# Smaller weight units, Silu in one instruction and a third seven-product pair in the feed-forward of a two-layer trunk

## The chip, the cores and the metric

The kernel runs on one core of a Trainium2 chip. The metric is the device time of one execution in microseconds (us), the median of several runs. The engines of the core work side by side, each through its own queue in order: TensorE (PE: matmuls; PEld: the loading of the stationary operand, which overlaps them), VectorE (DVE), ScalarE (ACT), GpSimd (POOL) and SyncE (SP), whose queue issues nearly all transfers from memory here.

## The reference

A decoder trunk of two layers over 256 tokens, width 2048, everything in 32-bit floats. Layer 0 mixes by an mLSTM and a Mamba-2 group, layer 1 by attention; each is followed by the same kind of feed-forward, which the change concerns:

```python
D_MODEL, SEQ = 2048, 256
D_FF = (8 * D_MODEL + 3 * 256 - 1) // (3 * 256) * 256      # 5632

def swiglu(x, w_gate, w_up, w_down):
    return (jax.nn.silu(x @ w_gate) * (x @ w_up)) @ w_down

for layer in range(DEPTH):
    xn = rms_norm(x, norm_mix[layer])
    if layer % 2 == 0:
        x = x + mixer_mlstm_ssd(xn, *mixer_params[layer])
    else:
        x = x + mixer_moba(xn, *mixer_params[layer])
    x = x + swiglu(rms_norm(x, norm_ffn[layer]), *ffn_params[layer])
return rms_norm(x, final_norm)
```

## The kernel before

**Numbers.** TensorE gets its operands in a reduced 32-bit form (`F32R`). Each operand is split into a high part (a cast, on ScalarE) and a low part (operand minus high part, a subtraction on VectorE), and each product is made of three matmuls: high x high, high x low, low x high (`add`, lines 396 to 398). Weights go through this too: a raw tile lands in memory on chip, ScalarE writes `wh`, VectorE writes `wl` (lines 368 and 370).

**Tiling of the feed-forward.** The 5632 hidden columns are 11 strips of 512. They go in parts of 4, 4 and 3 strips. For each strip of a part, `hidden` makes gate and up (one *hidden block*), applies the gate and turns the result over by transposes into `hT`. After the strips of a part, `down` multiplies `hT` with the matching rows of the down weights and adds into the residual `xr_`, in two *down blocks* (q = 0 and 1) of 1024 output columns each.

**Pairs.** A block (`block`) runs over pairs of 128-row tiles of the weights: 8 pairs in a hidden block and in a down block of a four-strip part, 6 in a down block of the three-strip part. A pair multiplies two halves of the tokens (128 each) with two strips of 512 columns over two row tiles: a 2 x 2 by 2 x 2 block product. A letter in a plan says how a pair is done. `P`, plain: 8 products, 24 matmuls into four PSUM banks `F`. `S`, seven products (Strassen-Winograd): 21 matmuls, some into `F`, some into four further banks `E`. It needs sums and differences of the four weight tiles (lines 377 to 380, on VectorE) and of the activations (`activation_sums`), each with its own split. The plans before are `PLAN_X` = PSPSPSPP for hidden blocks, PSPSPPPP and PSPSPP for down blocks of parts of 4 and 3 strips. After the last S of a block the four `E` banks are combined on VectorE into `pre`; in a hidden block `F` is then added to it, in a down block both are added to the residual (line 870).

**Buffers.** `weights` takes units from rings: a unit holds four weight tiles (one pair over two strips), 8 KB in each of the 128 partitions. There are four raw units and three each of `wh` and `wl`. A seven-product pair takes two raw units (one for the sums) and two of `wh` and `wl`, a plain pair one of each. A unit is used again when its last reader is through; the transfer into a raw unit, on SP's queue, waits for that.

**The gate.** Silu is made as tanh on ScalarE (line 857) and two VectorE instructions (858, 859), with the normalization's factor in them.

**Order.** Each engine's instruction order is fixed when the program is built, from the order of the code and from priorities (`tc.high_priority`). Deferred work (`later`, `tick`), such as the transposes of a hidden strip, runs after a pair, and not between the first and the last S of a block (`held`), when the `E` banks are taken.

## Time and profile before

| What | us |
|---|---|
| median of 3 runs (2606.25 to 2607.76) | 2606.94 |
| profiled execution, first to last instruction | 2605.5 |
| TensorE busy in it | 2577.1 |
| VectorE busy | 2043.3 |
| ScalarE busy | 1422.6 |
| feed-forward of layer 0, about 790 to 1500 | 710 |
| feed-forward of layer 1, about 1890 to 2595 | 705 |

The profiled execution is 1.4 us shorter than the median. In the rows of the profile "idle before" is the time in which an engine stood, and the arrow names what ended it. `acc_f` and `acc_e` are the banks `F` and `E`, `x` and `skx` the activations of a hidden block and their sums, `ha` or `hb` and `skh` those of a down block (first and second layer). A view of stretches gives, for each stretch of time, the busy time and count of instructions of each engine, the granted TensorE clock, the share of the DMA engines and the rate.

### The profile page before, as it was taken

How to read it: one execution, taken by the hardware profiler on the slowest of the kernel's cores; microseconds unless marked ns; L12 is line 12 of the kernel's file. 1: busy time of each engine (PE TensorE's matmuls, PEld its weight loads, DVE VectorE, ACT ScalarE, POOL GpSimd, SP SyncE). 2: the span in 40 equal slices, each digit the busy share in tenths (PEclk: the TensorE clock that was granted, in tenths of full speed). 3: DMA queues.
4: the chain of work that ended last, by engine and by line, in shares of the span. 5: the costliest groups of instructions: out<-in, count | busy, mean ns of one | idle time of the engine just before them, and what ended most of it. 6: DMA issues, size and time to landing. Idle time of an engine off the chain costs nothing.

```text
span 2605.5 us, 32598 instructions
## 1 busy us (share of the span) xinstructions
PE 2577.1 (99%) x12255; PEld 2143.7 (82%) x12255; DVE 2043.3 (78%) x2568; ACT 1422.6 (55%) x1886; POOL 46.9 (2%) x97
## 2 busy tenths in 40 slices
PE   8999999999999999999999999999999999999998
PEld 7888888888887888888888788888888888888886
DVE  6676777755548998899889865666699988998898
ACT  5466665565445654555455555566555545554554
POOL 2000010000000000000000000000000000000000
PEclk9999999999999999999999999999999999999999
DMA  7566676566655566565656455555556555565554
GB/s 228 177 184 185 178 236 189 167 186 214 189 173 192 196 200 206 176 216 189 209 173 215 162 170 177 178 171 180 191 173 223 189 199 186 202 215 184 200 193 153
DMA packets 254766, 496.66 MB, mean 191 GB/s; under 512 B 15705, under 2 KB 16097, under 8 KB 254353
## 3 DMA queue, kind: packets, MB, share of 16 engines
q1 hardware_dynamic: 250816, 484.57, 57.6%
q0 software_dynamic: 2896, 8.51, 1.2%
q8 instruction: 96, 1.57, 0.2%
q10 hardware_dynamic: 896, 1.52, 0.2%
q14 instruction: 62, 0.50, 0.1%
HBM read 492.39 MB, written 2.14 MB: 190 GB/s over the span
## 4 chain that ended last, share of the span: by engine, by line
PE 96%; DVE 2%; DMA 1%; ACT 1%; issue 0%; SPq 0%; POOL 0%; ACTq 0%; POOLq 0%; DVEq 0%
PE acc_f L397 14%; PE acc_f L396 14%; PE acc_f L398 14%; PE acc_w L305 11%; PE acc_a L347 8%; PE acc_a L349 8%; PE acc_a L348 8%; PE acc_w L309 6%; PE acc_e L396 3%; PE acc_e L397 3%; PE acc_e L398 3%; PE p_tr L223 2%; PE p_y L776 1%; DMA raw<-in_l_ffn_down 0%; PE p_num L653 0%; DVE wl L290 0%
## 5 line engine op out<-in xcount | busy, mean ns | idle before, releaser
L290 DVE TENSOR_TENSOR wl<-raw,wh 128x1024 fp32r<-128x1024 f32 (+1 forms) x385 | 469.7, 1220 | 335.1 <-ACT wh L289 331.1
L368 ACT CAST wh<-raw 128x1024 fp32r<-128x1024 f32 (+1 forms) x438 | 480.0, 1139 | 345.6 <-PE acc_f L398 284.7
L370 DVE TENSOR_TENSOR wl<-raw,wh 128x1024 fp32r<-128x1024 f32 (+1 forms) x438 | 571.7, 1329 | 66.7 <-ACT wh L368 64.2
L289 ACT CAST wh<-raw 128x1024 fp32r<-128x1024 f32 (+1 forms) x385 | 403.1, 1047 | 389.6 <-PE acc_a L349 172.9
L397 PE MATMUL acc_f<-wl,x 128*128 128x512 f32 x1012 | 394.4, 390 | 0.5 <-DVE wl L370 0.4
L398 PE MATMUL acc_f<-wh,x 128*128 128x512 f32 x1012 | 394.7, 390 | 0.0
L396 PE MATMUL acc_f<-wh,x 128*128 128x512 f32 x1012 | 393.1, 391 | 1.1 <-ACT wh L368 1.1
L368 ACT CAST wh<-sums 128x1024 fp32r<-128x1024 f32 x180 | 183.4, 1051 | 152.9 <-PE acc_f L398 115.4
L370 DVE TENSOR_TENSOR wl<-sums,wh 128x1024 fp32r<-128x1024 f32 x180 | 214.9, 1219 | 17.3 <-ACT wh L368 17.0
L397 PEld LDWEIGHTS acc_f<-wl,x 128*128 128x128 f32 x1012 | 190.0, 188 | 42.0 <-DVE wl L370 2.6
L396 PEld LDWEIGHTS acc_f<-wh,x 128*128 128x128 f32 x1012 | 189.7, 188 | 41.4 <-ACT wh L368 2.8
L398 PEld LDWEIGHTS acc_f<-wh,x 128*128 128x128 f32 x1012 | 190.0, 188 | 38.7
L305 PE MATMUL acc_w<-xa,wh 128*128 128x512 f32 x768 | 209.3, 400 | 1.1 <-DVE xa L169 1.1
L305 PEld LDWEIGHTS acc_w<-xa,wh 128*128 128x128 f32 x768 | 140.1, 190 | 27.4 <-ACT wh L289 1.5
L347 PE MATMUL acc_a<-wh,xa 128*128 128x512 f32 x384 | 151.3, 394 | 0.0
L349 PE MATMUL acc_a<-wh,xa 128*128 128x512 f32 x384 | 150.9, 393 | 0.0
L348 PE MATMUL acc_a<-wl,xa 128*128 128x512 f32 x384 | 149.9, 390 | 0.0
L305 PE MATMUL acc_w<-x,wh 128*128 128x512 f32 x512 | 138.8, 401 | 0.0
L309 PE MATMUL acc_w<-xa,wl 128*128 128x256 f32 x768 | 121.6, 282 | 0.0
L377 DVE TENSOR_TENSOR sums<-raw 128x1024 f32<-128x1024 f32 x90 | 109.7, 1219 | 14.4 <-DMA raw<-in_l_ffn_up 9.4
L309 PEld LDWEIGHTS acc_w<-xa,wl 128*128 128x128 f32 x768 | 110.0, 190 | 6.6
L396 PE MATMUL acc_f<-wh,ha 128*128 128x512 f32 x280 | 109.7, 392 | 1.7 <-DVE xres L870 1.7
(320 smaller groups left out, 4554.2 us busy)
## 6 DMA issues: line engine op xcount, KB each, us to landing
raw<-in_l_w_in SPq DMA_DIRECT2D x191, 512.0 KB, 3.7
raw<-in_l_ffn_gate SPq DMA_DIRECT2D x176, 512.0 KB, 3.9
raw<-in_l_ffn_up SPq DMA_DIRECT2D x176, 512.0 KB, 4.8
raw<-in_l_ffn_down SPq DMA_DIRECT2D x176, 512.0 KB, 5.1
raw<-in_l_w_qkv SPq DMA_DIRECT2D x96, 512.0 KB, 3.6
raw<-in_l_w_out SPq DMA_DIRECT2D x64, 512.0 KB, 4.6
raw<-in_l_w_o SPq DMA_DIRECT2D x32, 512.0 KB, 4.7
rows<-scr POOLq DMA_DIRECT2D x10, 512.0 KB, 6.0
```

The source lines that it names most:

```text
L289: nc.scalar.copy(wh[:, ks, :], raw[:, ks, :])
L290: nc.vector.tensor_sub(wl[:, ks, :], raw[:, ks, :], wh[:, ks, :].bitcast(F32))
L305: nc.tensor.matmul(banks[f], wh[:, kk, f * P:(f + 1) * P], kt.both(k0 + kk), start=k0 + kk == 0, stop=False, skip_group_check=True)
L309: nc.tensor.matmul(banks[f][:, :T], wl[:, kk, f * P:(f + 1) * P], kt.parts(k0 + kk)[0], start=False, stop=k0 + kk == nk - 1, skip_group_ch ...
L347: nc.tensor.matmul(banks[t], xh[:, ts], wh[:, kk, :], start=k == 0, stop=False)
L348: nc.tensor.matmul(banks[t], xh[:, ts], wl[:, kk, :], start=False, stop=False)
L349: nc.tensor.matmul(banks[t], xl[:, ts], wh[:, kk, :], start=False, stop=k == nk - 1)
L368: nc.scalar.copy(h[:, c, :], of[:, c, :])
L370: nc.vector.tensor_sub(l[:, c, :], of[:, c, :], h[:, c, :].bitcast(F32))
L396: nc.tensor.matmul(dst, ah, bh, start=start, stop=False)
L397: nc.tensor.matmul(dst, ah, bl, start=False, stop=False)
L398: nc.tensor.matmul(dst, al, bh, start=False, stop=stop)
```

## The change

Three things at once. Weight units hold one strip of two tiles instead of two strips: twice as many units of half the size (`FFN`). A plain pair takes two of them in turn, each cast and split by itself. A seven-product pair takes four raw units (`a`, `b`, `sums`, `last`): the fourth difference is made in place in `b`, and the last sum stands alone in `last`. The order of the products is changed a little (2, 1, 3 instead of 2, 3, 1), and a plain pair works through both token halves of the first strip before the second strip. Silu is one ScalarE instruction, followed by one on VectorE. And `PLAN_H[4]` has a third S, for which `skh` gets a third buffer; the place comes from the gains of the last norm, which now lie in pairs in a buffer of the `small` ring.

```diff
-PLAN_H = {4: "PSPSPPPP", 3: "PSPSPP"}
+PLAN_H = {4: "PSPSPSPP", 3: "PSPSPP"}
...
-FFN = ({"raw0": 2}, {"wh0": 1}, {"wl0": 1}, {"raw1": 2, "wh1": 2, "wl1": 2}, {"skh": 2}, {"gf": 2}, {"blk": 4})
+FFN = ({"raw0": 4}, {"wh0": 2}, {"wl0": 2}, {"raw1": 4, "wh1": 4, "wl1": 4}, {"skh": 3}, {"blk": 4})
...
-            return held_tile(kind + ring[turn[kind] % len(ring)], [P, 4, STRIP], name, dt)
-
-        raw = unit("raw", "0011", "raw")
-        for i, (w, col) in enumerate(src):
-            nc.sync.dma_start(raw[:, 2 * i:2 * i + 2, :],
-                              w[row:row + 2 * P, col:col + STRIP].rearrange("(a p) f -> p a f", p=P))
-
-        def parts(of, cuts):
-            h = unit("wh", "011", "wh", F32R)
-            l = unit("wl", "011", "wl", F32R)
-            for c in cuts:
-                nc.scalar.copy(h[:, c, :], of[:, c, :])
-            for c in cuts:
-                nc.vector.tensor_sub(l[:, c, :], of[:, c, :], h[:, c, :].bitcast(F32))
-            return h, l
-
+            return held_tile(kind + ring[turn[kind] % len(ring)], [P, 2, STRIP], name, dt)
+
+        def parts(of, n=2):
+            h = unit("wh", "001111", "wh", F32R)
+            l = unit("wl", "001111", "wl", F32R)
+            nc.scalar.copy(h[:, :n, :], of[:, :n, :])
+            nc.vector.tensor_sub(l[:, :n, :], of[:, :n, :], h[:, :n, :].bitcast(F32))
+            return [(h[:, i, :], l[:, i, :]) for i in range(n)]
+
+        raw = []
+        for w, col in src:
+            raw.append(unit("raw", "00001111", "raw"))
+            nc.sync.dma_start(raw[-1], w[row:row + 2 * P, col:col + STRIP].rearrange("(a p) f -> p a f", p=P))
         with tc.high_priority(offset=800):
             if not summed:
-                return parts(raw, (slice(0, 2), slice(2, 4)))
-            sums = unit("raw", "0011", "sums")
-            nc.vector.tensor_sub(sums[:, 0:2, :], raw[:, 2:4, :], raw[:, 3:0:-2, :])
-            nc.vector.tensor_sub(sums[:, 2, :], raw[:, 2, :], sums[:, 1, :])
-            first = parts(raw, (slice(0, 3),))
-            nc.vector.tensor_sub(sums[:, 3, :], raw[:, 0, :], sums[:, 2, :])
-            return first + parts(sums, (slice(0, 2), slice(2, 4)))
+                return [parts(r) for r in raw]
+            a, b = raw
+            sums = unit("raw", "00001111", "sums")
+            last = unit("raw", "00001111", "last")
+            nc.vector.tensor_sub(sums[:, 0, :], b[:, 1, :], a[:, 1, :])
+            b21, b11 = parts(a)
+            nc.vector.tensor_sub(b[:, 1, :], b[:, 0, :], b[:, 1, :])
+            nc.vector.tensor_sub(sums[:, 1, :], b[:, 0, :], sums[:, 0, :])
+            b22, t3 = parts(b)
+            nc.vector.tensor_sub(last[:, 0, :], a[:, 0, :], sums[:, 1, :])
+            t1, t2_ = parts(sums)
+            t4, = parts(last, 1)
+            return b21, b11, b22, t3, t1, t2_, t4
...
-                for p in (2, 3, 1, 7, 5, 6, 4):
+                for p in (2, 1, 3, 7, 5, 6, 4):
...
-                for i in range(4):
+                for i in (0, 2, 1, 3):
...
-        rh = cst.tile([P, NT], F32, tag="rh", name="rh" + name)
-        rr = cst.tile([P, NT], F32, tag="rr", name="rr" + name)
-        nc.vector.tensor_scalar(rh, r, 0.5, None, op0=OP.mult)
-        nc.vector.tensor_mul(rr, rh, r)
...
-                nc.scalar.activation(h, g, AF.Tanh, scale=rh[:, t:t + 1])
-                nc.vector.scalar_tensor_tensor(h, h, 1.0, g, op0=OP.add, op1=OP.mult)
-                nc.vector.scalar_tensor_tensor(h, u, rr[:, t:t + 1], h, op0=OP.mult, op1=OP.mult)
+                nc.scalar.activation(h, g, AF.Silu, scale=r[:, t:t + 1])
+                nc.vector.scalar_tensor_tensor(h, u, r[:, t:t + 1], h, op0=OP.mult, op1=OP.mult)
...
-        gain[s] = held_tile("gf", [P, STRIP], "gf")
+        if s % 2 == 0:
+            gain["pair"] = small([P, 2, STRIP], "gf")
+        gain[s] = gain["pair"][:, s % 2, :]
```

The built order moves at two places of which the prediction speaks. The first is VectorE at the start of the last down block of the first layer. Before, from the split of its first plain pair (`wl<-raw` x2) on; the first `sums<-raw` begins the block's first seven-product pair, the second its second one:

```order
L370 TENSOR_TENSOR wl<-raw,wh 128x1024 x2
L377 TENSOR_TENSOR sums<-raw 128x1024
L370 TENSOR_TENSOR wl<-raw,wh 128x1536
L378 TENSOR_TENSOR sums<-raw,sums 128x512
L870 TENSOR_TENSOR xres_5689<-xres_5689,pre 128x512
L380 TENSOR_TENSOR sums<-raw,sums 128x512
L870 TENSOR_TENSOR xres_5689<-xres_5689,acc_f 128x512
L377 TENSOR_TENSOR sums<-raw 128x1024
L370 TENSOR_TENSOR wl<-sums,wh 128x1024 x2
```

After, from the first seven-product pair's first difference to the second one's:

```order
L376 TENSOR_TENSOR sums<-raw 128x512
L363 TENSOR_TENSOR wl<-raw,wh 128x1024
L865 TENSOR_TENSOR xres_5689<-xres_5689,acc_f 128x512
L378 TENSOR_TENSOR raw<-raw 128x512
L379 TENSOR_TENSOR sums<-raw,sums 128x512
L865 TENSOR_TENSOR xres_5689<-xres_5689,pre 128x512
L363 TENSOR_TENSOR wl<-raw,wh 128x1024
L865 TENSOR_TENSOR xres_5689<-xres_5689,acc_f 128x512
L381 TENSOR_TENSOR last<-raw,sums 128x512
L363 TENSOR_TENSOR wl<-sums,wh 128x1024
L363 TENSOR_TENSOR wl<-last,wh 128x512
L376 TENSOR_TENSOR sums<-raw 128x512
```

The low parts of the first pair's sums (`wl<-sums`) stood behind the second pair's `sums<-raw`; now they and `wl<-last` stand ahead of it.

The second is ScalarE at the end of the first hidden block of layer 0. Before:

```order
L428 COPY pre<-acc_e 128x512
L368 CAST wh<-raw 128x1024 x4
L368 CAST wh<-raw 128x1536
L857 ACTIVATE h<-pre,rha 128x512 x2
L368 CAST wh<-sums 128x1024 x2
```

After:

```order
L429 COPY pre<-acc_e 128x512
L362 CAST wh<-raw 128x1024 x6
L853 ACT_TABLE_LOAD
L853 ACTIVATE h<-pre,r_6983 128x512 x2
L362 CAST wh<-raw 128x1024
L362 CAST wh<-sums 128x1024
L362 CAST wh<-last 128x512
```

A table load stands ahead of the first Silu. There are two more: at the first exponential of the attention and at the first Silu of layer 1.

More of the change, by code (lines that the diff above doesn't have):

```diff
@@ L68, in hybrid_trunk @@
     pad2 = ctx.enter_context(tc.tile_pool(name="pad2", bufs=1))
-    pad2.tile([P, 32], F32, name="pad2")
+    pad2.tile([P, 48], F32, name="pad2")
     psm = ctx.enter_context(tc.tile_pool(name="psm", bufs=1, space=PSUM))
@@ L405, in block @@
                 held[0] = True
-                wh, wl, sh, sl = weights(src, row + 2 * j * P, True)
+                b21, b11, b22, t3, t1, t2_, t4 = weights(src, row + 2 * j * P, True)
                 tok = lambda k, t: tuple(x[:, t * P:(t + 1) * P] for x in kt.parts(k))
@@ L411, in block @@
                 s1, s2, s3, s4 = [(sk[:, i, 0, :], sk[:, i, 1, :]) for i in range(4)]
-                b21, b11, b22 = [(wh[:, i, :], wl[:, i, :]) for i in range(3)]
-                t3, t1, t2_, t4 = [(sh[:, i, :], sl[:, i, :]) for i in range(4)]
                 prod = {1: (a11, b11), 2: (a12, b21), 3: (s4, b22), 4: (a22, t4),
                         5: (s1, t1), 6: (s2, t2_), 7: (s3, t3)}
-                for p in (2, 3, 1, 7, 5, 6, 4):
+                for p in (2, 1, 3, 7, 5, 6, 4):
                     if p in (2, 3, 4):
@@ L443, in block @@
                         F[i] = bank(i, "acc_f")
-                    for jj, (wh, wl) in group:
+                    for jj, w in group:
                         for kk in range(2):
@@ L447, in block @@
                             ts = slice(t * P, (t + 1) * P)
-                            add(F[i], (xh[:, ts], xl[:, ts]), (wh[:, 2 * s + kk, :], wl[:, 2 * s + kk, :]),
+                            add(F[i], (xh[:, ts], xl[:, ts]), w[s][kk],
                                 start=first and jj == group[0][0] and kk == 0, stop=jj == n - 1 and kk == 1)
```

## The prediction

> **What bounds the kernel now.** I read the head of the profile first, then the table of busy time by stretch, then TensorE's rows in order of time, then the waits. All times are microseconds.
>
> ```profile
> PE 2577.1 (99%) x12255; PEld 2143.7 (82%) x12255; DVE 2043.3 (78%) x2568; ACT 1422.6 (55%) x1886; POOL 46.9 (2%) x97
> ```
>
> TensorE is busy for 99% of the 2605.5 us span, but VectorE's 78% is a mean over unlike stages, so the feed-forward has to be looked at by itself. Four consecutive kinds of block of the first layer (a first down block of a four-strip part, a second one, a hidden block, a first down block of the three-strip part):
>
> ```profile
> core 0: us, PE busy (x) PEld busy (x) DVE busy (x) ACT busy (x) POOL busy (x), PEclk, DMA share, GB/s
> 1217.20:1260.70 43.50, 43.50 (x196) 35.55 (x195) 39.68 (x45) 20.75 (x22) 0.00 (x0) 1.00 0.61 198
> 1260.70:1302.80 42.10, 42.10 (x187) 34.90 (x186) 33.88 (x37) 19.49 (x19) 0.00 (x0) 1.00 0.60 200
> 1344.30:1387.00 42.70, 42.70 (x193) 34.98 (x192) 40.22 (x47) 24.19 (x26) 0.00 (x0) 1.00 0.58 197
> 1429.70:1462.30 32.60, 32.60 (x147) 26.46 (x146) 30.72 (x35) 17.06 (x18) 0.00 (x0) 1.00 0.59 192
> ```
>
> TensorE never pauses in these, at full granted clock. VectorE is 94% busy in a hidden block and 91% and 80% in the two down blocks: second in line, and close. The pace of TensorE is read between two rows of one unbroken run, 50 matmuls apart:
>
> ```profile
> 1450.76 0.39 PE L396 MATMUL acc_f<-wh,ha 128*128 128x512 f32 x1
> ...
> 1462.09 0.39 PE L398 MATMUL acc_f<-wh,ha 128*128 128x512 f32 x1
> ```
>
> 11.33 / 50 = 0.2266 per matmul (the 0.39 in the rows is one matmul's latency; they overlap). Who waits for whom says the same: ScalarE's splits wait for TensorE to give weight buffers back, not the reverse.
>
> ```profile
> ACT wh L368 <- PE acc_f L398: 400.1, 166, 5.7
> PE acc_f L396 <- DVE xres L870: 1.7, 1, 1.7
> PE acc_e L397 <- DVE wl L370: 1.1, 2, 0.9
> PE acc_e L396 <- ACT wh L368: 0.5, 1, 0.5
> PE acc_f L396 <- ACT wh L368: 1.1, 2, 0.9
> PE acc_f L397 <- DVE wl L370: 0.4, 1, 0.4
> PEld p_tr L223 <- DVE h L859: 5.9, 21, 0.4
> ```
>
> The first and the last three rows are of the whole run, the other three of 1425 to 1500, the end of the first layer's feed-forward. TensorE's matmuls wait 1.7 + 1.1 + 0.5 = 3.3 there, most of what they wait in both feed-forwards. So the feed-forward is bound by the number of matmuls, with one visible hole.
>
> **The third seven-product pair.** A plain pair is 4 banks x 2 tiles x 3 matmuls = 24, a seven-product pair 7 x 3 = 21. The four-strip parts have two down blocks each, two parts, two layers: 8 blocks, one pair changed in each, 8 x 3 = 24 matmuls less. 24 x 0.2266 = **5.44 off the path**. This is the one certain term, as long as the other engines keep up.
>
> What it asks of the others, from groups split by shape (mean ns after the busy time):
>
> ```profile
> L370 DVE TENSOR_TENSOR wl<-raw,wh 128x1024 fp32r<-128x1024 f32 x348 | 414.6, 1219 | 53.4 <-ACT wh L368 52.9
> L370 DVE TENSOR_TENSOR wl<-sums,wh 128x1024 fp32r<-128x1024 f32 x180 | 214.9, 1219 | 17.3 <-ACT wh L368 17.0
> L370 DVE TENSOR_TENSOR wl<-raw,wh 128x1536 fp32r<-128x1536 f32 x90 | 157.8, 1753 | 13.3 <-ACT wh L368 11.2
> L377 DVE TENSOR_TENSOR sums<-raw 128x1024 f32<-128x1024 f32 x90 | 109.7, 1219 | 14.4 <-DMA raw<-in_l_ffn_up 9.4 <-DMA raw<-in_l_ffn_down 4.2 <-PE acc_a L349 0.7
> L378 DVE TENSOR_TENSOR sums<-raw,sums 128x512 f32<-128x512 f32 x90 | 61.6, 684 | 0.2
> L858 DVE SCALAR_TENSOR_TENSOR h<-h,pre 128x512 f32<-128x512 f32 x44 | 29.8, 684 | 0.0
> L252 DVE TENSOR_TENSOR sf<-xg,sf 128x128 f32<-128x128 f32 x18 | 5.3, 292 | 0.6
> L870 DVE TENSOR_TENSOR xres<-xres,pre 128x512 f32<-128x512 f32 x48 | 32.0, 683 | 0.2 <-ACT pre L428 0.2
> ```
>
> VectorE pays for a seven-product pair 1.219 + 2 x 0.684 + 1.753 + 2 x 1.219 = 6.78 now. After the change it is three 1024-wide splits, and five 512-wide instructions (four differences and the split of the single last one): 3 x 1.219 + 5 x 0.684 = 7.08, 0.30 more. A plain pair stays 2 x 1.219 = 2.44. A changed down block gains 2 x 0.30 + 7.08 - 2.44 = 5.24. The activation sums of the new pair are four 0.29 steps and a 0.68 split, 1.8, once in a part's third hidden block.
>
> **Silu.** It takes one 0.684 instruction (L858) out of each half of a hidden block: 2 x 0.684 = 1.37, against 3 x 0.30 added there. A hidden block goes from 40.22 to 39.8 of 42.7. A first down block, in whose window its strip's elementwise tail falls, goes to 39.68 + 5.24 - 1.37 = 43.6, where TensorE now needs 43.50 - 3 x 0.2266 = 42.8; a second down block to 33.88 + 5.24 = 39.1 of 41.4. The first is over by 0.8, but the two together need 82.7 of 84.2, hidden blocks on both sides leave 2.9 each, and these are durations, which overlap in back-to-back instructions. With a prepared pair ahead the 0.8 doesn't reach TensorE: I take 0. Without that cover it is 4 x 0.8 = 3.2.
>
> Silu and the exponential of the attention need other table loads: the built order has three more than before. The trace has one load:
>
> ```profile
> 2.15 1.28 ACT L458 ACT_TABLE_LOAD   x1 [2.15 <-issue]
> ```
>
> Three are 3.85 on ScalarE. Behind each stand the Silu (or the exponential) itself and the next casts, for which VectorE's splits and then TensorE wait. ScalarE is busy 24.2 of a hidden block's 42.7, and one plain pair held ready is 24 x 0.2266 = 5.4 of TensorE work, four times a load. So the price lies between 0 and 3.85; I take 0.6, near the covered end.
>
> [...]
>
> **Units of one strip.** Same bytes in twice the number of buffers, so nothing is added to the traffic. A buffer comes free after the products that read it: after 6 of a seven-product pair's 21 matmuls for the first pair of tiles, where it was 9 for the first tile and 21 for the sums. Plain pairs take both token halves of a strip first, so the second strip is needed after 12 matmuls, not 6. This can only make arrivals earlier, except that more instructions stand in each queue. What it can win is the hole shown above; its rows on VectorE, with the transfer that it waits for from the chain:
>
> ```profile
> 1455.69 2.35 DVE L370 TENSOR_TENSOR wl<-raw,wh 128x1024 fp32r<-128x1024 f32 x2
> 1457.96 1.22 DVE L377 TENSOR_TENSOR sums<-raw 128x1024 f32<-128x1024 f32 x1
> ...
> 1462.58 0.67 DVE L870 TENSOR_TENSOR xres<-xres,acc_f 128x512 f32<-128x512 f32 x1
> 1464.85 1.23 DVE L377 TENSOR_TENSOR sums<-raw 128x1024 f32<-128x1024 f32 x1 [1.59 <-DMA raw<-in_l_ffn_down]
> 1465.99 2.35 DVE L370 TENSOR_TENSOR wl<-sums,wh 128x1024 fp32r<-128x1024 f32 x2
> ```
>
> ```profile
> 1458.48 6.24 DMA raw<-in_l_ffn_down
> ```
>
> The plain pair's split ends at 1458.04 and frees the raw buffer; its refill is issued at 1458.48 and lands at 1464.72. VectorE has 5.2 of work meanwhile, then stands at the second pair's sums, behind which the first pair's own low parts (1465.99) and the residual additions are queued, for which TensorE waits. In the new order the first pair's low parts stand ahead of the second pair's sums. Between the freeing split and those sums stand five 0.68 steps, three 1.22 splits and three residual additions of 0.683: 3.4 + 3.7 + 2.0 = 9.1, more than the transfer's 6.24 and its 0.4 of issue. So the landing is hidden and nothing urgent queues behind it. I take all 3.3; the ends are 0 (another transfer late next) and, if the waits on splits and on the hidden strips go too, 3.3 + 1.1 + 0.4 + 5.9 = 10.7, of which the 5.9 are weight-load waits mostly under a running matmul.
>
> The gains of the last norm move into a buffer of the activation sums; four short transfers, off the path.
>
> **Sum.** Against the profiled span: 2605.5 - 5.44 - 3.3 + 0.6 = 2597.4. The median of the timed runs, 2606.94, lies 1.4 above that span; the same sum against it gives **2598.8**, 0.31% less. About 0.2% (5.2 us) is what can be told from no change.
>
> **Rivals.**
> 1. Products only: the hole stays, or another landing is late in the new order. For: the order is fixed in advance, and VectorE queues strictly. Against: 9.1 of work over 6.24. 2606.94 - 5.44 = 2601.5, at the edge of what can be told. 0.20.
> 2. The table loads land on the path, each with its own 1.28: 2606.94 - 8.74 + 3.85 = 2602.1. For: a load stands in the queue ahead of casts. Against: the buffered pair. 0.12. [...]
> 3. VectorE becomes the bound in the first down blocks, the slower case. Its idle 43.50 - 39.68 = 3.8 there would have to be handoffs that cannot be filled, not slack from TensorE; then a block takes 43.6 + 3.8 = 47.4 instead of 42.8, 4.6 each in four blocks, 18.4: 2606.94 - 8.74 + 18.4 = 2616.6. It decides once the idle that stays passes 1.2 a block: 4 x (0.8 + 1.2) = 8.0 is all that is won. Against: the 400.1 of ScalarE waiting for TensorE, and unpaused TensorE at 94% in hidden blocks. 0.08.
> 4. Finer units close the other holes too: 2606.94 - 5.44 - 10.7 = 2590.8 at most, 2594 if half of the rest goes. 0.10.
>
> **Chances.** The forecast itself has 0.50, in 2596 to 2601.5. Faster by over 0.2% (under 2601.7) takes nearly all of the forecast (0.48), all of 4, about half of 1 and a little of 2: 0.71. Slower is 3 alone: 0.08. Within 0.2%: 0.21. The range from 2593.5 to 2605 leaves out 3, the far end of 4 and a tenth of the rest.
>
> **What would show it.** TensorE: 24 matmuls fewer, still unpaused in hidden and down blocks, at 0.2266. The eight changed down blocks end 0.68 sooner each. No wait on VectorE at a sum of the last down block of the first layer, no matmul wait over 0.3 there. Three more table loads, with no matmul idle within 6 us behind them (rival 2 if there is). VectorE near 98% in first down blocks but with TensorE still full; if TensorE waits for low parts there, rival 3. It is wrong if the hole has moved, or if VectorE's idle in those blocks stays near 3.8 while they grow longer.

## The result: slower, and the profile after

| | predicted | measured |
|---|---|---|
| time, us | 2598.8 (2593.5 to 2605.0) | 2629.26 (2625.66 to 2630.54) |
| against the kernel before in the same runs, 2607.35 us | 0.9969 | 1.0077 (1.0064 to 1.0089) |
| profiled execution, us (before 2605.5) | 2597.4 | 2628.8 |

The changed kernel is 21.9 us slower where 8 us less were forecast. The head of its page, the row that answers to the prediction's first:

```profile
PE 2581.6 (98%) x12231; PEld 2141.4 (81%) x12231; DVE 2069.3 (79%) x2768; ACT 1470.6 (56%) x2003; POOL 46.8 (2%) x97
```

TensorE has the 24 matmuls less (12255 to 12231), and yet the span is 23.3 longer. Where that lies is read from block to block: the length of a block is the time from the start of its first product to the start of the next block's first. In the feed-forwards the four-strip parts have a first down block, a second one, and a hidden block of the next part behind them. Over the four such parts these three add up to 508.2 us before and 530.9 after: 22.7 of the 23.3. All other stretches together hold the small rest: the end of layer 0's feed-forward and what follows it up to layer 1's is 4.5 shorter, the other blocks are about as much longer in sum. The view of stretches for the changed kernel, with the three of layer 0's second part (first down, second down, hidden), then the second down block and the hidden block of layer 1's first part:

```profile
1223.50:1267.80 44.30, 43.10 (x193) 34.88 (x192) 39.92 (x49) 24.00 (x27) 0.00 (x0) 1.00 0.63 201
1267.80:1314.30 46.50, 43.47 (x184) 35.25 (x183) 37.82 (x46) 21.54 (x23) 0.00 (x0) 0.96 0.52 168
1314.30:1356.50 42.20, 41.90 (x184) 34.09 (x183) 38.10 (x47) 22.58 (x26) 0.00 (x0) 1.00 0.64 215
2112.40:2155.90 43.50, 42.50 (x184) 33.96 (x184) 36.58 (x44) 20.49 (x22) 0.00 (x0) 1.00 0.64 209
2155.90:2202.10 46.20, 43.79 (x184) 35.44 (x185) 40.98 (x50) 24.88 (x27) 0.00 (x0) 0.96 0.56 188
```

The last two of these in the kernel before:

```profile
2105.20:2147.40 42.20, 42.20 (x188) 34.95 (x187) 34.40 (x37) 19.49 (x19) 0.00 (x0) 1.00 0.60 200
2147.40:2188.90 41.50, 41.50 (x185) 34.37 (x184) 34.71 (x35) 21.71 (x21) 0.00 (x0) 1.00 0.61 203
```

Before, TensorE fills each of them. After, it should need 183 x 0.2266 = 41.5 in every one of the last two kinds and takes up to 46.5. The first down blocks, in which the prediction looked for trouble, have grown least: their mean over the four parts goes from 43.4 to 43.9, that of the second ones from 42.2 to 44.6, that of the hidden blocks behind them from 41.5 to 44.2. And VectorE is not busy all the time in the long ones: it has 8.7 us idle in the 46.5.

What TensorE waits for in the changed kernel, and what ScalarE and VectorE wait for in the feed-forward:

```profile
PE acc_f L399 <- DVE xres L865: 8.1, 12, 2.1
PE p_tr L223 <- DVE h L854: 5.9, 8, 1.1
PE acc_f L400 <- DVE wl L363: 5.3, 4, 3.0
...
ACT wh L362 <- DMA raw<-in_l_ffn_down: 26.1, 8, 4.9
DVE sums L376 <- DMA raw<-in_l_ffn_down: 21.9, 11, 4.2
```

Before, the first was 1.7 and the last 4.2 (in 3 times); casts that wait for down weights were not among the waits at all. The first row names the largest: `xres` at line 865 is the addition of a down block's banks into the residual. Until it is done the next block cannot have the bank. By place the growth has three strands. In layer 1 the hidden blocks behind the second down blocks wait for banks and take 4.7 and 4.6 more. In layer 0 the second down blocks wait for low parts (third row) and take 1.5 and 4.4 more. And in layer 0 the first down blocks wait at transposes (2.4 of the second row) and take 1.9 and 0.8 more. In the twelve blocks the waits for `xres` are 7.9 in sum, those for `wl` 5.3.

**The closing work of a block has moved past the block's end.** Rows for the additions into the residual at the end of one down block, those of the `F` banks (`acc_f`) and those of the combined `E` banks (`pre`). Before (the block ends at 2147.4; the first of the four `pre`, at 2124.4, lies ahead of the view):

```profile
L870 DVE TENSOR_TENSOR xres<-xres,acc_f x4: 677/679/689, 2143.5 to 2148.1; 128x512 f32<-128x512 f32 x4
L870 DVE TENSOR_TENSOR xres<-xres,pre x3: 682/683/686, 2131.9 to 2137.1; 128x512 f32<-128x512 f32 x3
```

After (the block ends at 2155.9):

```profile
L865 DVE TENSOR_TENSOR xres<-xres,pre x4: 685/688/695, 2145.8 to 2173.1; 128x512 f32<-128x512 f32 x4
L865 DVE TENSOR_TENSOR xres<-xres,acc_f x4: 680/684/687, 2155.1 to 2174.8; 128x512 f32<-128x512 f32 x4
```

Before, the last one begins 0.7 after the block's end; after, 18.9 after it (in layer 0 it is 13). The `E` banks can only be combined after the last S of the plan. With PSPSPPPP that is the fourth pair of eight, and four combinations and the four additions of what they give, 8 x 0.68, spread over the four plain pairs behind it (4 x 24 x 0.2266 = 21.8 us). With PSPSPSPP it is the sixth, and the same eight have two pairs, 10.9 us, in which VectorE also has the splits and the next block's sums. The four additions of the `F` banks come with the last pair in both; in the changed kernel they are queued among the others. The 11 us before and the 10 us behind this border, in the kernel before and then in the changed one:

```profile
2136.40:2147.40 11.00, 11.00 (x51) 9.09 (x50) 8.25 (x11) 3.49 (x3) 0.00 (x0) 1.00 0.54 185
2147.40:2157.40 10.00, 10.00 (x46) 8.28 (x45) 8.15 (x9) 5.49 (x5) 0.00 (x0) 1.00 0.33 107
```

```profile
2144.90:2155.90 11.00, 10.62 (x47) 8.47 (x46) 11.00 (x14) 4.96 (x6) 0.00 (x0) 1.00 0.80 255
2155.90:2165.90 10.00, 7.92 (x27) 6.08 (x28) 8.81 (x13) 3.94 (x5) 0.00 (x0) 0.83 0.08 28
```

VectorE goes from 75% to 100% of the last 11 us, with TensorE waiting behind it: 27 matmuls fall into the 10 us that held 46.

**Idle and late in the same block.** The 5 us for which VectorE stood earlier in this block are part of it. VectorE's row in order of time, then ScalarE's, then TensorE's at the border:

```profile
2143.29 2.60 DVE L363 TENSOR_TENSOR wl<-raw,wh 128x1024 fp32r<-128x1024 f32 x2 [5.02 <-ACT wh L362]
...
2158.76 0.68 DVE L865 TENSOR_TENSOR xres<-xres,acc_f 128x512 f32<-128x512 f32 x1
```

```profile
2142.21 1.05 ACT L362 CAST wh<-raw 128x1024 fp32r<-128x1024 f32 x1 [4.95 <-DMA raw<-in_l_ffn_down]
```

```profile
2157.13 0.39 PE L401 MATMUL acc_f<-wh,x 128*128 128x512 f32 x1
2159.59 0.57 PE L399 MATMUL acc_f<-wh,x 128*128 128x512 f32 x1 [2.07 <-DVE xres L865]
```

VectorE waits for a cast, the cast for a transfer of down weights. Transfers stood in SP's queue for want of a free raw unit, and raw units come free when VectorE has split them: SP waits up to 7.9 for `wl` between 2124 and 2140 (total, times, longest),

```profile
SPq L369 <- DVE wl L363: 11.9, 4, 7.9
```

while the DMA engines had little to do (share 0.27) before they were full (1.05):

```profile
2127.00:2132.00 5.00, 5.00 (x23) 4.14 (x23) 3.26 (x6) 3.17 (x3) 0.00 (x0) 1.00 0.27 93
...
2141.00:2146.00 5.00, 5.00 (x23) 3.92 (x22) 2.56 (x3) 3.47 (x5) 0.00 (x0) 1.00 1.05 393
```

I read this as one chain: VectorE, late from the first down block's closing work, frees raw units late, idles until they are filled, and lacks at the next border what it lost there. The runs below show the ends of this chain; its middle, the raw units, they leave open.

### The profile page after: what moved, and what is told of

Its sections match the earlier page's. It is cut to its first block, busy times and chain, and to the rows that moved or that the text cites. A ratio compares the mean times of both kernels' runs of the same rounds, so it can differ in the third digit from the quotient of the medians.

```text
span 2628.8 us, 33211 instructions
## 1 busy us (share of the span) xinstructions
PE 2581.6 (98%) x12231; PEld 2141.4 (81%) x12231; DVE 2069.3 (79%) x2768; ACT 1470.6 (56%) x2003; POOL 46.8 (2%) x97
## 4 chain that ended last, share of the span: by engine, by line
PE 74%; DVE 14%; DMA 6%; issue 4%; ACT 2%; SPq 0%; DVEq 0%; POOL 0%; ACTq 0%; POOLq 0%
PE acc_w L305 11%; PE acc_f L400 8%; PE acc_f L401 8%; PE acc_f L399 8%; PE acc_a L347 8%; PE acc_a L349 8%; PE acc_a L348 8%; DVE wl L363 7%; PE acc_w L309 6%; DMA raw<-in_l_ffn_down 3%; DMA raw<-in_l_ffn_up 3%; PE acc_e L399 2%; PE acc_e L401 2%; PE acc_e L400 2%; ACT wh L362 1%
## 5 line engine op out<-in xcount | busy, mean ns | idle before, releaser
L362 ACT CAST wh<-raw 128x1024 fp32r<-128x1024 f32 x528 | 546.0, 1053 | 416.8 <-PE acc_f L401 190.5
L290 DVE TENSOR_TENSOR wl<-raw,wh 128x1024 fp32r<-128x1024 f32 (+1 forms) x385 | 470.0, 1221 | 334.2 <-ACT wh L289 330.1
L363 DVE TENSOR_TENSOR wl<-raw,wh 128x1024 fp32r<-128x1024 f32 x528 | 636.7, 1223 | 86.0 <-ACT wh L362 82.7
L289 ACT CAST wh<-raw 128x1024 fp32r<-128x1024 f32 (+1 forms) x385 | 403.1, 1047 | 388.9 <-PE acc_a L349 175.7
L305 PEld LDWEIGHTS acc_w<-xa,wh 128*128 128x128 f32 x768 | 140.1, 190 | 27.3 <-ACT wh L289 1.5
L363 DVE TENSOR_TENSOR wl<-sums,wh 128x1024 fp32r<-128x1024 f32 x98 | 119.9, 1223 | 3.7 <-ACT wh L362 3.2
L362 ACT CAST wh<-sums 128x1024 fp32r<-128x1024 f32 x98 | 102.7, 1048 | 15.3 <-PE acc_e L401 7.8
L305 PEld LDWEIGHTS acc_w<-x,wh 128*128 128x128 f32 x512 | 93.3, 189 | 17.7
L362 ACT CAST wh<-last 128x512 fp32r<-128x512 f32 x98 | 60.8, 620 | 82.5 <-DVE last L381 59.1
```

Source lines behind the costliest of these rows:

```text
L289: nc.scalar.copy(wh[:, ks, :], raw[:, ks, :])
L290: nc.vector.tensor_sub(wl[:, ks, :], raw[:, ks, :], wh[:, ks, :].bitcast(F32))
L305: nc.tensor.matmul(banks[f], wh[:, kk, f * P:(f + 1) * P], kt.both(k0 + kk), start=k0 + kk == 0, stop=False, skip_group_check=True)
L362: nc.scalar.copy(h[:, :n, :], of[:, :n, :])
L363: nc.vector.tensor_sub(l[:, :n, :], of[:, :n, :], h[:, :n, :].bitcast(F32))
```

## The experiments

All times are ratios to the kernel before in the same runs, with the 95% interval. "Parts add up" is the product of what the single edits gave.

### Each edit by itself

The kernel before with the third pair alone (units of two strips, tanh), and with the third buffer and the moved gains that it needs:

```diff
-PLAN_H = {4: "PSPSPPPP", 3: "PSPSPP"}
+PLAN_H = {4: "PSPSPSPP", 3: "PSPSPP"}
...
```

> The kernel before with only the third seven-product pair in the down blocks of the four-strip parts (24 matmuls less), with the third buffer for the activation sums and the gains of the last norm moved as in the change. Old units, old order of products, tanh. Theory VECTOR (the third pair's extra work on VectorE makes it late in and around the down blocks): the 5.4 us are lost and more, 2610 to 2622. Theory UNITS (the one-strip units, whose in-place difference makes ScalarE's cast wait for VectorE, are what stalls TensorE): 2600 to 2603, the matmuls come back in full. Theory ORDER (a plain pair's new order asks for a bank's residual addition sooner): 2600 to 2603 too.

1.0032 (1.0020 to 1.0045). With 24 matmuls fewer, 5.4 us, it is 8 us slower. The additions into the residual end 7.8 to 11.5 us behind the border here too, but TensorE hardly waits for banks because of it: the one wait of a matmul for `xres` is the old hole, and the new waits are for casts and, in the first down blocks, for activations.

```profile
PE acc_f L396 <- ACT wh L368: 2.9, 6, 0.9
...
PE acc_f L396 <- DVE xres L870: 1.7, 1, 1.7
```

The kernel before with Silu alone:

```diff
-nc.scalar.activation(h, g, AF.Tanh, scale=rh[:, t:t + 1])
-nc.vector.scalar_tensor_tensor(h, h, 1.0, g, op0=OP.add, op1=OP.mult)
-nc.vector.scalar_tensor_tensor(h, u, rr[:, t:t + 1], h, op0=OP.mult, op1=OP.mult)
+nc.scalar.activation(h, g, AF.Silu, scale=r[:, t:t + 1])
+nc.vector.scalar_tensor_tensor(h, u, r[:, t:t + 1], h, op0=OP.mult, op1=OP.mult)
```

> The kernel before with only Silu in place of tanh and the first of the two VectorE instructions. All theories of the stall that do not blame Silu: 2602 to 2608, VectorE 30 us less busy, the hole at the end of the first layer's feed-forward somewhat smaller. Theory SILU (table loads, or the gate's result reaching the transposes later): 2610 or more, with matmul waits at the hidden strips' transposes.

0.9986 (0.9977 to 0.9995): a gain, table loads and all.

The changed kernel with tanh and with two S in the plan, that is units of one strip alone, and the same kernel once more in a later set of runs:

```diff
-PLAN_H = {4: "PSPSPSPP", 3: "PSPSPP"}
+PLAN_H = {4: "PSPSPPPP", 3: "PSPSPP"}
...
-nc.scalar.activation(h, g, AF.Silu, scale=r[:, t:t + 1])
+nc.scalar.activation(h, g, AF.Tanh, scale=rh[:, t:t + 1])
```

> The changed kernel with tanh and without the third pair: the units of one strip and the new orders alone, against the kernel before. Theory UNITS: 2620 to 2635, most of the loss is here. Theory VECTOR: 2603 to 2610, since VectorE has only 0.3 us a seven-product pair more. Theory ORDER: about 2615, 8 us from waits for banks at the starts of blocks after down blocks.

> The units of one strip with the tanh gate and without a third pair once more, beside the run above: 0.9982 again, and 0.0005 more than that run if the two matter-of-count gains add up.

0.9982 (0.9972 to 0.9992) and 0.9984 (0.9975 to 0.9993). Silu alone and units alone, by some 4 us each, are the only kernels here that are faster than the kernel before by more than their interval. Neither is the culprit by itself.

### Two edits of three

The changed kernel without the third pair, and the changed kernel with tanh (the two halves of the diff above):

> The changed kernel with the plan of before (two seven-product pairs in those down blocks, 24 matmuls more): one-strip units and Silu stay. Theory THIRD (the third pair, put on the one-strip units, is what stalls TensorE): the small gains of the units (0.18% alone) and of Silu (0.14% alone) add up, 2599 to 2605, no matmul wait over 1 us in the four-strip parts. Theory PAIRING (units and Silu disturb each other without the third pair): 2612 or more.

> The changed kernel with tanh and its two VectorE instructions: units and third pair stay. Theory THIRD with VectorE short of time: 1.4 us more VectorE work a hidden block makes it worse than the changed kernel, 2630 to 2642. Theory SILU (the gate's place in ScalarE's order or the table loads bring the loss): 2605 to 2618.

Without the third pair 1.0012 (1.0003 to 1.0021), with tanh 1.0075 (1.0058 to 1.0092). Both results lie between what the two readings expected. The third pair carries nearly all of the loss, Silu none of it beside the third pair. But the pair's price hangs on the units: 0.32% on units of two strips, 0.65% on units of one strip with Silu and 0.9% with tanh. Why finer units make it dearer, no run here shows.

Units and Silu together should have given 0.9968 and gave 1.0012, 11 us more. One place is common to the kernels with both: the first down block of the last part of layer 1 takes 34.4 to 36.7 us in place of 32.4. In the changed kernel the transposes of the last hidden strip stand there behind 24 and 45 of the block's matmuls (61 and 66 with units alone), and wait 1.1 and 0.6 for `h`. With Silu alone they stand behind 24 and 29, and nothing waits: Silu has moved them forward, and with the finer units VectorE gets there later. That is some 2.5 of the 11 us; where the others lie wasn't traced.

### Order, placement and GpSimd

The changed kernel with the old order in plain pairs:

```diff
-                for i in (0, 2, 1, 3):
+                for i in range(4):
```

> The changed kernel with the plain pairs' old order (both strips of the first token half, then of the second), the rest of the change kept. Theory ORDER: 8 us faster than the changed kernel (2629), about 2620, the waits of acc_f for the residual additions (8.1 us now) back under 2. Theories UNITS and VECTOR: 2626 to 2632.

1.0115 (1.0096 to 1.0134), slower than any reading expected: in this kernel the new order is worth 10 us, and it is not the cause.

The changed kernel with the fourth difference not in place but in `last`, beside the last sum. VectorE's order changes with it, and so does that of the products:

```diff
-            nc.vector.tensor_sub(b[:, 1, :], b[:, 0, :], b[:, 1, :])
             nc.vector.tensor_sub(sums[:, 1, :], b[:, 0, :], sums[:, 0, :])
-            b22, t3 = parts(b)
-            nc.vector.tensor_sub(last[:, 0, :], a[:, 0, :], sums[:, 1, :])
+            b22, = parts(b, 1)
             t1, t2_ = parts(sums)
-            t4, = parts(last, 1)
+            nc.vector.tensor_sub(last[:, 0, :], b[:, 0, :], b[:, 1, :])
+            nc.vector.tensor_sub(last[:, 1, :], a[:, 0, :], sums[:, 1, :])
+            t3, t4 = parts(last)
...
-                for p in (2, 1, 3, 7, 5, 6, 4):
+                for p in (2, 1, 3, 5, 6, 7, 4):
```

> The changed kernel, with the difference that is made in place in the second raw unit put beside the last sum instead, so that ScalarE's cast of that unit waits for its transfer alone and no longer for VectorE; same count of VectorE instructions, products in the order 2, 1, 3, 5, 6, 7, 4. Theory INPLACE (ScalarE standing 90.9 us behind that difference is what makes low parts late): 2603 to 2618. Theory VECTOR (VectorE is late by itself around the down blocks, ScalarE only follows): 2624 to 2634.

1.0161 (1.0146 to 1.0176): 22 us worse than the changed kernel, and outside of both readings. The loss does not go with the in-place difference; what that difference costs by itself the run can't say, since two orders changed with it. Equal work in other orders costs as much again as the whole change.

The changed kernel with the additions of the combined `E` banks into the residual on GpSimd, in all twelve down blocks:

```diff
-                def add_all(what):
+                def add_all(what, eng=nc.vector):
                     for d, x in zip(dst, what):
-                        nc.vector.tensor_add(d, d, x)
+                        eng.tensor_add(d, d, x)
+
+                def add_sums(what):
+                    add_all(what, nc.gpsimd)
...
```

> The changed kernel with the first four residual additions of each down block (those of the combined banks) on GpSimd: 2.7 us less for VectorE in each of the 12 down blocks, same arithmetic. Theory VECTOR: a good part of the loss comes back, 2605 to 2620. Theory INPLACE: little, 2622 to 2632. [...]

1.0027 (1.0015 to 1.0039): 13 of the 20 us come back. At the border of the same block as above (it ends at 2150.8 here) VectorE's additions are done 3 us behind the end in place of 19, and TensorE's waits for `xres` fall from 8.1 to 1.1 in the whole run:

```profile
L865 DVE TENSOR_TENSOR xres<-xres,acc_f x4: 672/674/676, 2148.5 to 2153.1; 128x512 f32<-128x512 f32 x4
```

```profile
PE acc_f L399 <- DVE xres L865: 1.1, 3, 0.5
```

The same edit without the third pair:

> The changed kernel without the third pair (measured 1.0012), with the first four residual additions of each down block on GpSimd. VECTOR as a threshold: VectorE has room there without them, so little is won, 0.999 to 1.001. VECTOR as a steady price for each us on VectorE in down blocks (4.8 us per block cost 20 us in eight blocks, 0.5 each; 2.7 us in twelve blocks): 0.995 to 0.997. PAIRING (each edit's fixed order costs some us by chance): anything from 0.997 to 1.003.

1.0041 (1.0026 to 1.0056), slower than without it (1.0012), and outside of what each reading expected. So GpSimd doesn't simply take load off VectorE. Groups split by shape, first without the edit, then with it:

```profile
L363 DVE TENSOR_TENSOR wl<-raw,wh 128x1024 fp32r<-128x1024 f32 x528 | 637.7, 1220 | 109.1 <-ACT wh L362 105.3
...
L376 DVE TENSOR_TENSOR sums<-raw 128x512 f32<-128x512 f32 x90 | 61.6, 685 | 25.4 <-DMA raw<-in_l_ffn_down 12.4 <-DMA raw<-in_l_ffn_up 12.3 <-PE acc_a L349 0.7
...
L865 DVE TENSOR_TENSOR xres<-xres,pre 128x512 f32<-128x512 f32 x48 | 32.1, 683 | 0.0
```

```profile
L865 POOL TENSOR_TENSOR xres<-xres,pre 128x512 f32<-128x512 f32 x48 | 90.8, 1912 | 1308.3 <-ACT pre L429 1257.5 <-DVE pre L431 46.1 <-PE acc_f L401 4.7
...
L363 DVE TENSOR_TENSOR wl<-raw,wh 128x1024 fp32r<-128x1024 f32 x528 | 657.0, 1258 | 105.0 <-ACT wh L362 100.7
...
L376 DVE TENSOR_TENSOR sums<-raw 128x512 f32<-128x512 f32 x90 | 69.6, 773 | 31.1 <-DMA raw<-in_l_ffn_down 15.7 <-DMA raw<-in_l_ffn_up 14.6 <-PE acc_a L349 0.7
```

VectorE is rid of 48 additions, 32.1 us, but its splits and differences of raw tiles are 19.3 + 8.0 = 27.3 us longer. Nearly all of the relief is paid back: VectorE is busy for 2032.6 us without the edit and 2033.8 with it. On the changed kernel it does give some, 2069.3 to 2058.9. I take the main part of the gain there to be that four additions no longer stand in VectorE's queue among the next block's splits; the runs don't part the two.

### Load, sums, and which down block

The changed kernel, its third pair (`special`) without the weight sums, so that what this pair adds up is another result:

```diff
+            if special:
+                b21, b11 = parts(a)
+                b22, t3 = parts(b)
+                return b21, b11, b22, t3, b21, b11, b22
```

> The changed kernel, where the third seven-product pair of each of the eight changed down blocks has no weight sums: its four combinations are left out (the products use the splits of the four weight tiles in their place, so the sum it makes is another), and VectorE spends 2 x 1.219 = 2.44 us on it as on a plain pair, not 7.08. TensorE has the same 24 matmuls fewer as the changed kernel; ScalarE's splits of the sums go too. VECTOR (the work of the sums is what costs): the 20 us come back, ratio 0.997 to 1.001. THIRD by its banks (four E banks held for two pairs longer, so that transposes and tails come late): it stays slow, 1.005 to 1.009.

1.0018 (1.0009 to 1.0028): most of the loss goes with the sums, but with 24 matmuls fewer it is still no faster than without the third pair at all (1.0012). Second down and hidden block:

```profile
2104.80:2147.50 42.70, 42.03 (x184) 34.19 (x183) 36.02 (x44) 20.28 (x21) 0.00 (x0) 1.00 0.61 197
2147.50:2189.40 41.90, 41.76 (x184) 34.29 (x183) 34.92 (x41) 22.66 (x25) 0.00 (x0) 1.00 0.58 181
```

VectorE's total is close to that of the kernel before (36.0 and 34.9 for 34.4 and 34.7), and TensorE pauses all the same, at both borders: the additions end 4.6 to 6.5 us late here. This part of the loss is not load. With the sums go two raw units and two casts a pair as well, so the run doesn't say which of these the larger part hangs on.

The counterpart, the load without the pair:

```diff
+            if special:
+                ...
+                parts(sums)
+                parts(last, 1)
+                return [wa, wb]
```

> The counterpart: plain third pair on TensorE (24 matmuls, no bank held longer, as in the changed kernel without its third pair, measured 1.0012), but the four differences and the splits of their sums are made all the same in those eight blocks, and nobody reads them: VectorE does 7.08 us for this pair, TensorE keeps its 24 matmuls. VECTOR: the load by itself costs, 1.006 to 1.010 (the changed kernel's 1.0077 plus up to 0.002 for the 24 matmuls that are not saved). THIRD by its banks: no more than 1.003.

1.0019 (1.0009 to 1.0028), 0.07% more than without that load. Second down and hidden block:

```profile
2105.70:2147.90 42.20, 42.20 (x188) 34.96 (x187) 38.69 (x47) 21.86 (x23) 0.00 (x0) 1.00 0.62 200
2147.90:2189.40 41.50, 41.50 (x185) 34.38 (x184) 33.65 (x39) 22.15 (x24) 0.00 (x0) 1.00 0.58 177
```

VectorE does 38.7 us in the second down block, more than the 36.6 of the changed kernel, and TensorE never pauses. "VectorE has too much to do", the theory with which these runs began, falls in that form: as many instructions cost next to nothing when the closing work stays behind the fourth pair, no product waits for them and no difference is made in place.

The third pair in the second down blocks alone, and in the first alone:

```diff
-hT, first * STRIP, 4 * n, PLAN_H[n], add_all,
+hT, first * STRIP, 4 * n, PLAN_H[n] if q or n == 3 else "PSPSPPPP", add_all,
```

> The changed kernel with the third seven-product pair in the second down block of each part alone (q = 1, four blocks, 12 matmuls fewer); the first ones, in which VectorE also finishes the last hidden strip, keep two. VECTOR as the prediction's third rival had it (first down blocks alone are too full): 0.998 to 1.001. VECTOR over the two blocks and the hidden block behind them together: half way between 1.0012 and 1.0077, 1.003 to 1.006.

> The mirror of the run with the third pair in the second down blocks alone: now in the first ones alone (q = 0, four blocks, 12 matmuls fewer). LOCAL (the first down block is too full by itself, as the prediction's third rival had it): the whole price stays, 20 us less 2.7, ratio 1.006 to 1.009, with first down blocks of 44 or more. RUN (VectorE's debt from the first down block is paid back in the second, where TensorE does 42.2 us of work to VectorE's 34 with two seven-product pairs, and both together are what is too much): the second down block drains it, 0.999 to 1.003, with second down blocks at 42.2 and the hidden blocks behind them at 41.5.

(For the first alone the condition is `not q or n == 3`.) 1.0002 (0.9992 to 1.0011) and 0.9996 (0.9987 to 1.0006). Neither costs anything; the loss needs both in a row. The second alone would have spoken for rival 3, that first down blocks are too full; only its mirror speaks against it. Both lie 0.0010 and 0.0016 below the kernel without a third pair (1.0012), about what 12 matmuls are worth (2.7 us), though the intervals overlap. First alone, second down and hidden block of layer 1's first part, then the same two with the second alone:

```profile
2107.40:2149.80 42.40, 42.40 (x188) 34.74 (x187) 38.50 (x47) 20.50 (x21) 0.00 (x0) 1.00 0.59 200
2149.80:2191.30 41.50, 41.50 (x185) 34.37 (x184) 34.59 (x40) 23.02 (x25) 0.00 (x0) 1.00 0.63 203
```

```profile
2104.20:2145.70 41.50, 41.50 (x185) 34.38 (x184) 35.04 (x41) 21.40 (x23) 0.00 (x0) 1.00 0.58 187
2145.70:2188.90 43.20, 42.34 (x185) 34.11 (x184) 38.68 (x47) 23.42 (x26) 0.00 (x0) 1.00 0.63 210
```

With the pair in the first block alone, its closing work runs 13 to 14 us into the second one, which in three of four parts takes 42.4 in place of 42.2 and hands on a hidden block without a pause (42.8 and a hidden block of 42.3 in the fourth). With the pair in the second alone, that block is 0.68 shorter, just 3 matmuls, its closing work runs 13 to 15 us into the hidden block, and that one gives back 0.2 to 1.8. So closing work that ends 13 to 15 us late costs little here, as in layer 0 of the changed kernel; at the two dear borders it ended 19.5 late. Lengths in us, means over the four parts:

| kernel | ratio | first down | second down | hidden behind |
|---|---|---|---|---|
| before | 1 | 43.4 | 42.2 | 41.5 |
| no third pair | 1.0012 | 43.8 | 42.2 | 41.5 |
| third pair in the first | 0.9996 | 43.4 | 42.5 | 41.7 |
| third pair in the second | 1.0002 | 44.0 | 41.5 | 42.5 |
| third pair in both (the change) | 1.0077 | 43.9 | 44.6 | 44.2 |
| both, without its sums | 1.0018 | 43.3 | 42.8 | 41.9 |
| its load alone | 1.0019 | 44.0 | 42.2 | 41.5 |

The ratios of the two single ones lie a little below what their block lengths alone would make (43.4 + 42.5 + 41.7 is 0.5 above before, which makes 2 us over four parts); blocks elsewhere differ by some us from kernel to kernel.

### In search of a better one

Units of one strip, tanh, and the third pair in the second down blocks; the same on the units of two strips with Silu; and the former with the third pair, and the activation sums for it, in layer 1 alone:

```diff
-PLAN_H[n] if q or n == 3 else "PSPSPPPP"
+PLAN_H[n] if n == 3 or (q and name == "b") else "PSPSPPPP"
...
```

> Units of one strip with the tanh gate (measured 0.9982 without a third pair) and the third pair in the second down blocks alone, which took 0.0010 off where Silu was in too. If the parts add up: 0.9972, and the first down block of the second layer's three-strip part stays at 32.4, where every kernel with units and Silu had 35.0. If each edit's fixed order costs some us by chance (PAIRING): 0.998 to 1.002.

> The kernel before (units of two strips) with Silu (measured 0.9986) and the third pair in the second down blocks alone (0.0010). If the parts add up: 0.9976. PAIRING: 0.998 to 1.002. If the third pair costs in the second block too with units of two strips, as it did in both blocks together (1.0032 alone): 1.000 to 1.003.

> Units of one strip with the tanh gate and the third pair in the second down blocks of the second layer alone (two blocks, 6 matmuls, 1.36 us). In the built order the transposes at the start of the second layer's feed-forward then stand behind 24 matmuls of its first hidden block, as without any third pair (there that block took 44.7), and not behind 3, as with a third pair in the first layer too (45.3 to 47.5). If that block's order is what took the gain back (PAIRING by place): 0.9982 less 0.0005, 0.9977, with that block at 44.7. If the third pair costs something else in that form: 0.999 to 1.001.

1.0000 (0.9990 to 1.0009), 1.0005 (0.9996 to 1.0015) and 0.9994 (0.9985 to 1.0003). The parts don't add up. In the first two the second layer's first hidden block took 47.5 and 47.8 (43.6 before, 44.7 with units alone); the transposes at its start stand behind 3 of its matmuls there, and behind 24 with units alone. That is not shown to be the cause: in the changed kernel they stand behind 2, and the block takes 43.1. The third keeps that block at 44.7, as expected, its two shortened down blocks are at 41.5, and the hidden blocks behind them take 42.7 and 42.3 in place of 41.5: the 0.68 saved is given back at once. In none of these kernels does a third pair at the sixth place win its 0.68 a block for certain; whether it would at an earlier place, with the closing work left where it was, wasn't tried.

### Raw units, left open

Is it the raw units that make VectorE late? The last sum in place of `a`'s first tile, three raw units a seven-product pair instead of four:

```diff
-            nc.vector.tensor_sub(last[:, 0, :], a[:, 0, :], sums[:, 1, :])
+            nc.vector.tensor_sub(a[:, 0, :], a[:, 0, :], sums[:, 1, :])
...
-            t4, = parts(last, 1)
+            t4, = parts(a, 1)
```

> The changed kernel, where the last sum of a seven-product pair is made in place, in the first tile of its raw unit a (already split by then), so that such a pair takes three raw units from the ring and not four: 19 units a changed down block in place of 22, of 8 in the ring. VectorE, ScalarE and TensorE have the same instructions of the same sizes. RAW (a weight transfer cannot start because VectorE is behind in freeing raw units; its late landing idles VectorE, which is then late with everything queued behind): fewer late landings, ratio 0.999 to 1.004, and the 26.1 us in which ScalarE's casts wait for down weights fall below 10. VECTOR (its work by itself is too much for the two blocks in a row): it stays at 1.006 to 1.009.

1.0127 (1.0110 to 1.0144). Both readings missed. The casts' waits for down weights are gone, but VectorE's sums still stand for them (last row; 21.9 in the changed kernel), and the kernel is 13 us slower than the changed one, with other waits:

```profile
PE p_tr L223 <- DVE h L853: 15.4, 21, 1.7
PE acc_e L399 <- DVE wl L363: 6.3, 5, 1.7
PE acc_f L399 <- DVE wl L363: 4.9, 5, 1.9
...
DVE sums L375 <- DMA raw<-in_l_ffn_down: 23.8, 14, 4.0
```

`a` is now held until the last split, and VectorE's order has changed with it. So the run moved the late transfers rather than removed them, and says nothing on what they cost; whether more raw units with the order unchanged would help is open and wasn't tried.

## Why the prediction was wrong, step by step

**The third pair's 5.44 off the path: right as a count, and worth nothing in the changed kernel.** 24 matmuls are gone, and where the pair stood alone in the second down block, that block was 0.68 shorter and unpaused. "As long as the other engines keep up" was the condition, and it did not hold.

**The step that failed: "With a prepared pair ahead the 0.8 doesn't reach TensorE: I take 0."** It set VectorE's work in two whole blocks, 82.7, against TensorE's 84.2. The runs show in its place a cost of some 28 us: the 22.7 by which the twelve blocks grew, and the 5.4 that they should have lost (1.5 of the 22.7 is there without the third pair too). Three things were wrong in it.
- The sum over blocks hid where in the block the work lies. The prediction counted what the third pair adds (5.24) and not what it moves: the combination of the `E` banks and the additions of the result, eight instructions, go from behind the fourth pair to behind the sixth. VectorE is at 100% in the last 11 us and at 88% in the 10 behind, with a mean of 84% in the block.
- 82.7 of 84.2 was taken as room. In layer 0's second part VectorE was busy for 39.9 + 37.8 = 77.7, less than the sum, and TensorE waited all the same. The load run shows that load of this size can be carried where nothing waits for it; where products wait for the sums, and banks for the closing work, it can't.
- The mark that the prediction itself set, idle time of VectorE that stays near 3.8 while blocks grow, came true in layer 0's second part: 4.4 idle in the first down block, which grew by 0.8, and 8.7 in the second. In the first, 3.6 of it is waiting for casts; in the second 4.4 for casts and 3.4 for a late transfer. None of it was slack to fill.

**Rival 3** (0.08; 2616.6) had the sign and the engine, not the place or the size. It put 4.6 on each first down block; they grew by 0.5, and the run with the third pair there alone shows that such a block is no bound. The debt passes to the blocks behind.

**The hole at the end of layer 0's feed-forward: right.** In the changed kernel TensorE waits once in 1425 to 1500, for another reason:

```profile
PE acc_e L399 <- DVE ha L166: 0.3, 1, 0.3
```

The units alone gave 4.2 to 4.7 us; 3.3 was taken. **Rival 1's** remark that another landing may be late in the new order also came true, in a four-strip part (last section).

**Silu: right, and the loads cheaper still.** Alone it gave 3.7 us. The first of the three new loads:

```profile
830.61 1.28 ACT L853 ACT_TABLE_LOAD   x1 [3.83 <-DVE pre L850]
```

Behind each of the three, no two matmuls start more than 0.24 us apart for 6 us: nothing of 0.6 arrived, and **rival 2** falls.

**The sum.** Terms were added that do not add. Units (0.9982), Silu (0.9986) and a third pair by its matmuls (0.9979) would give 0.9947, at the fast end of the stated range. Units and Silu together already lost 0.44% against their product, and the third pair 0.65% on top. At TensorE's 99% nothing stands in reserve, and each edit lets the scheduler write out another order for VectorE.

## What to carry to other kernels

Where an engine follows a fixed order, count what a change moves as well as what it adds: a pair that ends an accumulation later leaves all closing work to a shorter stretch, and a mean over the block will not show it; look at the second engine in the 10 us around each border. Test two neighbouring places of a change apart, since each may be free and both together not. And measure the edits one by one before they are joined: here two of three gained about 0.15% each, and the three together lost 0.77%.

## What the runs showed of the hardware

**Behind some pauses TensorE's matmuls start 0.43 apart for a while, and one pause of 2.07 has such starts behind it where another of 2.07 has none.** In the changed kernel, in layer 0's second part, behind a late landing. VectorE stands at a sum, with the `wl` behind it for which TensorE waits, just as in the old hole:

```profile
1283.02 0.69 DVE L376 TENSOR_TENSOR sums<-raw 128x512 f32<-128x512 f32 x1 [3.39 <-DMA raw<-in_l_ffn_down]
```

```profile
1285.51 0.50 PE L400 MATMUL acc_f<-wl,skh 128*128 128x512 f32 x1 [3.03 <-DVE wl L363]
...
1288.83 0.63 PE L399 MATMUL acc_f<-wh,ha 128*128 128x512 f32 x1
1289.26 0.47 PE L400 MATMUL acc_f<-wl,ha 128*128 128x512 f32 x1
```

The matmuls start 0.43 apart, not 0.2266; the granted clock of this block is 0.96, and 0.57 from 1285.5 to 1289.5. Three pauses in the changed kernel (3.03, 2.07 and 2.04) are followed by 6 or 7 such starts each, about 20 x 0.2 = 4.0 of the 23 us. But in the kernel without the third pair and with additions on GpSimd the same 2.07 is followed by none: from the second matmul behind it they start 0.23 apart:

```profile
1477.53 0.47 PE L399 MATMUL acc_e<-wh,skh 128*128 128x512 f32 x1 [2.07 <-DVE x L169]
1477.83 0.39 PE L400 MATMUL acc_e<-wl,skh 128*128 128x512 f32 x1
1478.06 0.40 PE L401 MATMUL acc_e<-wh,skh 128*128 128x512 f32 x1
```

What decides it, these runs do not show.

**With additions on GpSimd a part of VectorE's instructions takes longer.** An addition that takes VectorE 0.68 takes GpSimd 1.9. In the kernel without the third pair the first differences of raw tiles then take 0.773 in the mean in place of 0.685, and the splits of raw tiles 1.258 in place of 1.220; over the 48 additions that makes the 27.3 us, 0.57 each. VectorE's combinations, which read an `E` bank, stay at 0.68 in the mean. Why some take longer and others not, these runs do not show.
